# Hybrid decoder step on one core: in the second mixer, both background queues step together at every second tick up to the last head's products

## The chip, the cores and the metric

The kernel runs on one core of one Trainium2 chip. The metric is the device time of one execution in microseconds, the median of three runs. The engines are TensorE (PE in the profile; PEld is its weight load), VectorE (DVE), ScalarE (ACT), GpSimd (POOL) and SyncE (SP, which issues DMAs).

## The reference, cut to what matters

The program computes one inference step of a two-layer trunk of width 1024: layer 0 has a Mamba-2 mixer, layer 1 an HGRN2 mixer, each followed by a squared-ReLU MLP. 512 prompt tokens and 8 sequences of 4 new tokens pass through together, 544 columns in all. The change touches the second mixer, HGRN2, with 8 heads of 128 x 128:

```python
def hgrn_mixer(u, state, lb, w_in, norm_w, w_out):
    proj = (u @ w_in).astype(jnp.float32)
    q = jax.nn.silu(proj[..., :HGRN_F])
    fz = proj[..., HGRN_F:2 * HGRN_F]
    v = proj[..., 2 * HGRN_F:2 * HGRN_F + D_MODEL]
    g = proj[..., 2 * HGRN_F + D_MODEL:]
    logf = ...                                  # from fz and lb
    k = (1.0 - lb) * jax.nn.sigmoid(-fz)
    o, s = hgrn_chunk_scan(q, k, v, logf, state)   # S_t = diag(f_t) S_{t-1} + k_t v_t^T, o_t = S_t^T q_t
    o = group_rmsnorm(o, norm_w, HGRN_N_HEADS) * jax.nn.silu(g)
    return o @ w_out, s
```

## The kernel before, in words

Activations lie transposed, features on the 128 partitions and the 544 tokens along the free dimension. A big product is made in three fp32r passes (high and low halves of weight and activation), each as two matmuls of 272 columns; the weights come in units of 128 x 1024, are split into `whi` and `wlo` by `split` (L198: a cast on ScalarE, a subtraction on VectorE), and `products` (L319) writes them into one of two PSUM tiles `acc`. After every six steps (12 matmuls) `products` calls `tick` (L295).

In the second mixer (`hgrn`, L1175) the foreground is `head` (L1415) for h = 0 to 7: four products (q, f, v, g; four ticks each, so 16 ticks a head) and their evacuations. All the rest of a head is done in two background queues of Python generators, which `tick` advances:

- Queue 0, `levels` (L1231): seven levels s = 1, 2, 4, ... 64. Each issues small score products (`pa`, L1249, L1256, L1268), masks them into `ac` and `att` on VectorE, and multiplies q and K by decays on VectorE (L1279, L1280), which the next level's products read. Between two levels one step is `values` (L1305): transposes of v (`pv`, `pvs`). Each step yields `PACE_LEVELS`, so 8 steps a head.
- Queue 1, `states` (L1330), which `levels` starts when it ends: transposes of K (`pk`), the chunk states (`pS`, then S on VectorE, L1356), the old states' part (`pz`), the outputs (`po`, `pzs`; L1375 to L1380), their norm (squares on ScalarE, L1383; a sum, a Newton iteration of small steps and a scaling to `o2` on VectorE, L1386 to L1392), the two halves of the state update (`pn`, L1396, and four VectorE steps each on `hst`, L1399), the store of `hst`, and at the end transposes of `o2` (`pt`, `pts`; L1406, L1407), the gate `g` (L1410, L1411) and its split into `oh` and `ol`.

The numbers that a step yields are ticks until the next one: `tick` takes 1 from the first entry of each queue, and steps that queue while the entry is not above 0. The two queues keep their own time. Behind the last head come the products of the output projection, `pho` (L1456): half 0 of them reads the gated outputs of heads 0 to 3, half 1 those of heads 4 to 7, and `drain("hs7")` makes what is left of the last head's steps before half 1. They tick too, every 12 matmuls.

All small products share four PSUM tiles (`mx`). The framework below orders each engine's instructions by its own planning of the recorded program, so a matmul may stand a few places from where it was recorded; each engine then runs its list in order.

Of the kernel before, what the change touches and what calls it, by code (L numbers as in the profile page):

```python
# [41 lines left out]


PACE = (1.1, 0.9, 1.4, 0.8)
PACE_LEVELS, PACE_STATES = 1.8, 1.6

U_SSD_IN = 0
U_SSD_OUT = U_SSD_IN + 40
# [53 lines left out]
def trunk(ctx: ExitStack, tc: tile.TileContext, io):  # L102
# [37 lines left out]

    ready = {}
    loaded = {("u", i): t for i, t in enumerate(first)}
    state = {"load": 2, "conv": 0}
    loads = [("u", u) for u in range(U_MLP)]
    jobs = [(("u", u), u) for u in range(U_MLP)]

# [141 lines left out]
    def unit(u):  # L288
        return take(("u", u))
# [3 lines left out]
    queues = [[], []]  # L293

    def tick():  # L295
        for q in queues:
            if q:
                q[0][1] -= 1
                while q and q[0][1] <= 0:
                    step(q)  # L300

    def step(q):
        try:
            q[0][1] += next(q[0][0])
        except StopIteration:
            left = q.pop(0)[1]
            if q:
                q[0][1] += left
# [7 lines left out]
    def drain(name):  # L316
        for q in queues:
            while any(e[2] == name for e in q):
                step(q)  # L319
# [5 lines left out]
    def products(ps, w, ops, first, last, c0=0, step=P, run=0):  # L325

        n = len(ops)
        order = [(k, j) for k in range(n) for j in range(3)]
        run = run or (4 if "w" in sp else 0)
        if run:  # L330

            order = [(k, j) for k0 in range(0, n, run) for js in ((0, 1), (2,)) for k in range(k0, min(k0 + run, n)) for j in js]
        for i, (k, j) in enumerate(order):
            oh, ol = ops[k]
            a, o = ((w[0], oh), (w[0], ol), (w[1], oh))[j]
            for h in range(2):
                nc.tensor.matmul(  # L337
                    ps[:, h, :HF], block(a, c0 + k * step), o[:, h * HF : (h + 1) * HF],
                    start=(first and i == 0), stop=(last and i == len(order) - 1),
                )  # L340
            if i % 6 == 5:
                tick()

    def acc_tile(name):
        return psb.tile([P, 2, 512], F32, tag="acc", name=name)
# [79 lines left out]
    def add_to_x(m, ps, then):  # L425
        with tc.high_priority():
            nc.vector.tensor_tensor(v3(x[m]), ps[:, :, :HF], v3(x[m]), ADD)
        if then is not None:
            then(m)


    def ssd(then):
# [393 lines left out]
        def dt_product():  # L826

            wd = pool.tile([P, KT, NS], F32, tag="E", bufs=2, name="wd")
            nc.vector.tensor_tensor(
                wd, wdt, vec[:, V_NMIX0 : V_NMIX0 + KT].unsqueeze(2).to_broadcast([P, KT, NS]), MUL  # L830
            )
            pd = acc_tile("pd")
            for i in range(2):
                for h in range(2):
                    for c in range(4):
                        k = 4 * i + c
                        nc.tensor.matmul(
                            pd[c * NS : (c + 1) * NS, h, :HF], wd[:, k, :], x[k][:, h * HF : (h + 1) * HF],
                            start=(i == 0), stop=(i == 1), tile_position=(0, c * NS),
                        )  # L840
                tick()
            pdx = pool.tile([P, 640], F32, tag="xs", bufs=5, name="pdx")
            nc.vector.tensor_tensor(v3(pdx[:, :T]), pd[:, :, :HF], v3(rb), MUL)
            nc.gpsimd.tensor_copy(
                pdx[:, T:640].rearrange("p (a b) -> p a b", b=NS), pdx[:, NP_:T].unsqueeze(1).to_broadcast([P, 3, NS])
            )
            return pdx
# [122 lines left out]
    def mlp(name, plan, v0, then, last=False):  # L970
# [105 lines left out]
        def seventh(name_, u):  # L1076
# [11 lines left out]
            for k in range(4):  # L1088
                oh, ol = ops_[name_, k]
                for j, (w, o) in enumerate(((hi, oh), (hi, ol), (lo, oh))):  # L1090
                    nc.tensor.matmul(  # L1091
                        ps, block(w, k * P), o, start=(name_ in ("p1", "p2", "q7") and k == 0 and j == 0),
                        stop=(k == 3 and j == 2), skip_group_check=name_ in ("n6", "n5", "p3", "q4"),
                    )
            tick()
            release(1)
            keep = {"p1": "s1", "n6": "sv", "n5": "sw"}.get(name_)
# [81 lines left out]
    def hgrn(then):  # L1179
# [235 lines left out]
        def head(u, h):  # L1415
            hc = slice(h, h + 1)
            pq, pf = None, None
            if h == 0:
                pq, pf = product(u), product(u + 1)
                drain("hn")  # L1420
            qz = project(u, "qz", pq)
            QQ = pool.tile([P, 2, T], F32, tag="q", name=f"q{h}")
            q, Q = QQ[:, 0], QQ[:, 1]
            nc.scalar.activation(q, qz, AF.Sigmoid)
            nc.vector.tensor_tensor(q, qz, q, MUL)
            fz = project(u + 1, "fz", pf)
            f = pool.tile([P, T], F32, tag="f", name=f"f{h}")
            K = pool.tile([P, 640], F32, tag="K", name=f"K{h}")
            nf = pool.tile([P, T], F32, tag="nf", name=f"nf{h}")
            nc.scalar.activation(f, fz, AF.Sigmoid)  # L1430
            nc.scalar.activation(nf, fz, AF.Sigmoid, scale=-1.0)
            nc.vector.scalar_tensor_tensor(f, nf, lbf[:, hc], f, MUL, ADD)
            nc.vector.tensor_scalar(K[:, :T], nf, olb[:, hc], None, MUL)
            nc.vector.tensor_tensor(Q, q, f, MUL)
            d = {}
            background(levels(h, QQ, K, f, d), f"hl{h}", wait=2.5)
            d["vz"] = project(u + 2, "vz")
            gz = project(u + 3, "gz")
            g = pool.tile([P, T], F32, tag="g", name=f"g{h}")
            nc.scalar.activation(g, gz, AF.Sigmoid)  # L1440
            nc.vector.tensor_tensor(g, gz, g, MUL)
            d["g"] = g

        sc = slice(NP_, T)
        u = U_HGRN_IN
        ops = [[pool.tile([P, T], F32R, tag=f"o{c}{h}", bufs=1, name=f"o{c}{h}") for c in "hl"] for h in range(8)]
        for h in range(8):
            head(u, h)
            u += 4
        for half in range(2):  # L1450
            if half:
                drain("hs7")
            for mp in range(4):
                w = unit(u)
                u += 1
                for i in range(2):  # L1456
                    ps = acc_tile(f"pho{half}_{mp}_{i}")
                    products(ps, w, ops[4 * half : 4 * half + 4], True, True, i * P, 2 * P)
                    add_to_x(2 * mp + i, ps, then if half == 1 else None)
# [50 lines left out]
    ssd(pre_norm(V_NMLP0))  # L1510
    mlp("m0", plans[0], V_NMLP0, pre_norm(V_NMIX1))
    hgrn(pre_norm(V_NMLP1))
    mlp("m1", plans[1], V_NMLP1, last_norm, True)

# [111 lines left out]
def _build(arrays):  # L1626
    import concourse.bacc as bacc

    nc = bacc.Bacc("TRN2", target_bir_lowering=False, num_devices=1)
    io = {n: nc.dram_tensor(f"in_{n}", v.shape, mybir.dt.from_np(v.dtype), kind="ExternalInput").ap() for n, v in arrays.items()}  # L1630
    for n, s in _OUT.items():
        io[n] = nc.dram_tensor(f"out_{n}", s, F32, kind="ExternalOutput").ap()
    with tile.TileContext(nc) as tc:
        trunk(tc, io)
    return nc
# [22 lines left out]
```

## Time and profile before

| | |
|---|---|
| Median of 3 runs | 1518.32 us (1518.02 to 1518.69) |
| The profiled execution | 1517.97 us, its span 1516.2 us |
| TensorE busy over the span | 99% |
| VectorE busy over the span | 83% |
| Second mixer, first small product to last `pt` | 835 to 1123 us of the span |

The profiled execution is 0.35 us below the median. In the rows further down a time is the start in us from the beginning of the span; a row of the timeline merges instructions of the same kind that follow each other (x2 is a pair of 272-column matmuls). Ends of matmuls are modelled, so the starts are what is read.

### The profile page before, as it was taken

How to read it: one execution, taken by the hardware profiler on the slowest of the kernel's cores; microseconds unless marked ns; L12 is line 12 of the kernel's file. 1: busy time of each engine (PE TensorE's matmuls, PEld its weight loads, DVE VectorE, ACT ScalarE, POOL GpSimd, SP SyncE). 2: the span in 40 equal slices, each digit the busy share in tenths (PEclk: the TensorE clock that was granted, in tenths of full speed). 3: DMA queues.
4: the chain of work that ended last, by engine and by line, in shares of the span. 5: the costliest groups of instructions: out<-in, count | busy, mean ns of one | idle time of the engine just before them, and what ended most of it. 6: DMA issues, size and time to landing. Idle time of an engine off the chain costs nothing. (4 is left out here: it accounts for less than half of the span.)

```text
span 1516.2 us, 33224 instructions
## 1 busy us (share of the span) xinstructions
PE 1495.4 (99%) x13144; PEld 1440.3 (95%) x13144; DVE 1261.5 (83%) x2532; ACT 882.3 (58%) x1740; POOL 188.0 (12%) x273
## 2 busy tenths in 40 slices
PE   9999999999999999999999999999999999999997
PEld 7998989898999999999999999999999999999996
DVE  7879798978777989888898788888877989888895
ACT  5685766757346658575676333333336758576673
POOL 3211011110012111111110000000002111111101
PEclk9999999999999999999999999999999999999998
DMA  6366557574466667564754232233228666575741
GB/s 199 106 192 169 148 140 203 130 223 115 114 178 135 141 161 183 145 183 131 191 131 130 74 99 87 87 98 105 86 86 202 133 168 180 140 181 140 184 123 66
DMA packets 105789, 215.46 MB, mean 142 GB/s; under 512 B 16481, under 2 KB 36865, under 8 KB 105633
## 3 DMA queue, kind: packets, MB, share of 16 engines
q1 hardware_dynamic: 81328, 170.24, 34.7%
q0 software_dynamic: 23040, 41.95, 17.3%
q8 instruction: 103, 1.69, 0.5%
q10 hardware_dynamic: 1264, 1.14, 0.2%
q14 instruction: 54, 0.43, 0.1%
HBM read 196.12 MB, written 17.18 MB: 141 GB/s over the span
## 5 line engine op out<-in xcount | busy, mean ns | idle before, releaser
L199 ACT CAST whi<-raw 128x512 fp32r<-128x512 f32 x194 | 119.4, 617 | 212.0 <-PE ps L337 154.6
L200 DVE TENSOR_TENSOR wlo<-raw,whi 128x512 fp32r<-128x512 f32 x194 | 133.8, 691 | 30.8 <-ACT whi L199 28.0
L188 POOL DMA_DIRECT2D v<-in_W x94 | 83.0, 1038 | 463.6 <-DVE fl_p L200 134.0
L337 PE MATMUL ps<-uh_s,whi 128*128 128x272 f32 x576 | 124.3, 297 | 2.5 <-DVE BC L518 2.4
L337 PE MATMUL ps<-ul_s,whi 128*128 128x272 f32 x576 | 120.2, 290 | 0.0
L337 PE MATMUL ps<-uh,whi 128*128 128x272 f32 x512 | 112.6, 300 | 0.0
L337 PE MATMUL ps<-ul,whi 128*128 128x272 f32 x512 | 106.5, 289 | 0.0
L337 PE MATMUL ps<-uh,wlo 128*128 128x272 f32 x512 | 106.3, 289 | 0.0
L337 PEld LDWEIGHTS ps<-uh_s,whi 128*128 128x128 f32 x576 | 90.5, 189 | 8.5 <-issue 6.9
L337 PEld LDWEIGHTS ps<-ul_s,whi 128*128 128x128 f32 x576 | 90.9, 189 | 0.2
L200 DVE TENSOR_TENSOR fl_p<-raw,fh_p 128x512 fp32r<-128x512 f32 x94 | 64.1, 689 | 28.9 <-ACT fh_p L199 25.3
L337 PE MATMUL ps<-uh_s,wlo 128*128 128x272 f32 x576 | 86.4, 290 | 0.0
L337 PEld LDWEIGHTS ps<-uh,whi 128*128 128x128 f32 x512 | 80.8, 189 | 3.7 <-issue 1.4
L337 PEld LDWEIGHTS ps<-ul,whi 128*128 128x128 f32 x512 | 80.4, 189 | 0.0
L337 PEld LDWEIGHTS ps<-uh,wlo 128*128 128x128 f32 x512 | 80.0, 188 | 0.0
L199 ACT CAST fh_p<-raw 128x512 fp32r<-128x512 f32 x94 | 57.6, 620 | 37.9 <-PE pp L1091 19.9
L337 PEld LDWEIGHTS ps<-uh_s,wlo 128*128 128x128 f32 x576 | 78.1, 190 | 1.1 <-issue 0.8
L223 ACT CAST whi<-raw 128x512 fp32r<-128x512 f32 x66 | 40.6, 618 | 49.4 <-PE ps L337 19.6
L511 DVE SCALAR_TENSOR_TENSOR cacc<-pre,vh,cacc 128x568 f32<-128x568 f32 x72 | 57.8, 803 | 7.6 <-ACT cacc L509 7.1
L337 PE MATMUL po<-yh,whi 128*128 128x272 f32 x256 | 55.5, 297 | 1.2 <-ACT yh L199 1.2
L1091 PE MATMUL pp<-m_tl,fh_n 128*128 128x272 f32 x192 | 55.3, 288 | 0.0
L1091 PE MATMUL pc_q<-m_th,fh_q 128*128 128x272 f32 x192 | 55.3, 288 | 0.0
(480 smaller groups left out, 5156.0 us busy)
## 6 DMA issues: line engine op xcount, KB each, us to landing
raw<-in_W SPq DMA_DIRECT2D x175, 512.0 KB, 4.0
v<-in_W SPq DMA_DIRECT2D x94, 256.0 KB, 4.1
v<-in_W POOLq DMA_DIRECT2D x94, 256.0 KB, 5.6
wlo<-in_W POOLq DMA_DIRECT2D x66, 256.0 KB, 6.2
a<-in_W SPq DMA_DIRECT2D x47, 256.0 KB, 4.3
w<-cum_d SPq DMA_DIRECT2D x16, 512.0 KB, 6.9
st<-in_ssm_in SPq DMA_DIRECT2D x16, 512.0 KB, 4.6
out_ssm_s<-st SPq DMA_DIRECT2D x16, 512.0 KB, 6.6
```

Source lines behind the costliest of these rows:

```text
L188: nc.gpsimd.dma_start(raw[:, c : c + 512], io["W"][u + 1][:, :512], accum_op=ADD)
L199: nc.scalar.copy(hi, raw)
L200: (eng or nc.vector).tensor_tensor(lo, raw, hi.bitcast(F32), SUB)
L223: nc.scalar.copy(hi[a], c)
L337: nc.tensor.matmul(ps[:, h, :HF], block(a, c0 + k * step), o[:, h * HF : (h + 1) * HF], start=(first and i == 0), stop=(last and i == len( ...
L511: nc.vector.scalar_tensor_tensor(acc, pre[:, i : i + 568], vh[:, wc + 24 * i : wc + 24 * i + 1], acc, MUL, ADD)
L1091: nc.tensor.matmul(ps, block(w, k * P), o, start=(name_ in ("p1", "p2", "q7") and k == 0 and j == 0), stop=(k == 3 and j == 2), skip_group ...
```

## The change

`tick` counts its calls. A queue still loses 1 per tick, but is stepped only at ticks whose number is a multiple of `beat`. `beat` is 2 from the first head to the last head's own products, and 1 before and behind them. A step of `levels` now yields 2 instead of 1.8.

```diff
-PACE_LEVELS, PACE_STATES = 1.8, 1.6
+PACE_LEVELS, PACE_STATES = 2, 1.6
...
-    state = {"load": 2, "conv": 0}
+    state = {"load": 2, "conv": 0, "ticks": 0, "beat": 1}
...
     def tick():
+
+        state["ticks"] += 1
         for q in queues:
             if q:
                 q[0][1] -= 1
-                while q and q[0][1] <= 0:
+                while q and q[0][1] <= 0 and state["ticks"] % state["beat"] == 0:
                     step(q)
...
         u = U_HGRN_IN
+        state["beat"] = 2
         ops = [[pool.tile([P, T], F32R, tag=f"o{c}{h}", bufs=1, name=f"o{c}{h}") for c in "hl"] for h in range(8)]
         for h in range(8):
             head(u, h)
             u += 4
+        state["beat"] = 1
         for half in range(2):
```

The two programs hold the same instructions on every engine; their order differs from the mixer's first norm (`hn_pc`) on. Lines of the changed kernel are 2 higher than before for L296 to L1445 and 4 higher for what follows `head` in `hgrn`. A run of small products between two big matmuls is called a visit here. From the norm's `hn_pr` to the last `pt` PE's list has 97 visits before and 72 now.

**A head in the middle.** PE's list around the state steps of head 2 and the level steps of head 3 (the first digit in a name is the head's, the last number only counts tiles); first before:

```order
L1249 MATMUL pa3_2_12379<-q3_12194,K3_12284 32x32 x16
L1256 MATMUL pa3_2_12379<-q3_12194,K3_12284 32x32
L1352 MATMUL pS2_12406<-vt2_12120,kt2_12349 128x128 x4
...
L337 MATMUL ps134_12301<-uh7_16_10603,wlo134_1_12202 128x272 x2
L1362 MATMUL pz2_12429<-hst2_12342,qm2_12351 32x128 x8
L1365 MATMUL pz2_12429<-ident_77,K2_11776 128x128
L337 MATMUL ps135_12456<-uh0_16_10131,whi135_0_12293 128x272 x2
...
L1249 MATMUL pa3_4_12469<-q3_12194,K3_12284 32x32 x16
L1375 MATMUL po2_12491<-vt2_12120,att2_11842 128x128 x2
...
L1377 MATMUL po2_12491<-S2_12411,q2_11688 128x128
L1379 MATMUL pzs2_12499<-zi2_12439,h_sel_10632 32x128
L1380 MATMUL pzs2_12499<-vs2_12126,sats2_11843 32x128
L337 MATMUL ps135_12456<-uh2_16_10324,whi135_0_12293 128x272 x2
```

and in the changed kernel:

```order
L1251 MATMUL pa3_2_12428<-q3_12159,K3_12274 32x32 x16
L1258 MATMUL pa3_2_12428<-q3_12159,K3_12274 32x32
L1354 MATMUL pS2_12455<-vt2_12137,kt2_12385 128x128 x4
L339 MATMUL ps135_12403<-uh4_16_10475,whi135_1_12284 128x272 x2
...
L339 MATMUL ps135_12403<-uh7_16_10603,wlo135_1_12286 128x272 x2
L1251 MATMUL pa3_4_12490<-q3_12159,K3_12274 32x32 x16
L1364 MATMUL pz2_12512<-hst2_12378,qm2_12387 32x128 x8
L1367 MATMUL pz2_12512<-ident_77,K2_11753 128x128
L1377 MATMUL po2_12527<-vt2_12137,att2_11830 128x128 x2
...
L1379 MATMUL po2_12527<-S2_12460,q2_11638 128x128
L1381 MATMUL pzs2_12535<-zi2_12522,h_sel_10632 32x128
L1382 MATMUL pzs2_12535<-vs2_12143,sats2_11831 32x128
```

Before, `pz` is a visit of its own, 10 matmuls behind `pS`, and `po` follows 12 matmuls later together with the level's `pa`. Now `pa`, `pz`, `po` and `pzs` are one visit, 24 matmuls behind `pS`, and nothing but `po` stands between `pz` and `pzs`, which reads `zi`, ScalarE's copy of `pz`. All visits of the heads in the middle now have 24 matmuls between them.

**Behind the last head.** PE's list from the last state product of head 7 to the first use of its gated output `oh7`; first before:

```order
L1396 MATMUL pn7_1_15077<-vm7_14897,kq7_14972 128x512
L337 MATMUL pho0_3_1_15064<-oh2_10652,whi155_1_14903 128x272 x2
...
L1406 MATMUL pt7_15097<-ident_77,o27_14998 128x128 x4
L1407 MATMUL pts7_15098<-ident_77,o27_14998 128x32
L337 MATMUL pho1_0_0_15118<-oh4_10656,whi156_0_15024 128x272 x2
...
L337 MATMUL pho1_0_1_15149<-ol5_10659,whi156_0_15024 128x272 x2
L337 MATMUL pho1_0_0_15118<-oh7_10662,whi156_1_15025 128x272 x2
L337 MATMUL pho1_0_1_15149<-oh5_10658,wlo156_0_15026 128x272 x2
...
L337 MATMUL pho1_0_0_15118<-ol7_10663,whi156_1_15025 128x272 x2
L337 MATMUL pho1_0_0_15118<-oh7_10662,wlo156_1_15027 128x272 x2
```

and in the changed kernel:

```order
L339 MATMUL pho0_3_1_15024<-oh3_10654,wlo155_1_14882 128x272 x2
L1398 MATMUL pn7_0_15083<-vm7_14947,kq7_15020 128x512
L1398 MATMUL pn7_1_15090<-vm7_14947,kq7_15020 128x512
L339 MATMUL pho1_0_0_15118<-oh4_10656,whi156_0_14964 128x272 x2
...
L339 MATMUL pho1_0_1_15149<-oh6_10660,wlo156_1_14967 128x272 x2
L1408 MATMUL pt7_15097<-ident_77,o27_15048 128x128 x4
L1409 MATMUL pts7_15098<-ident_77,o27_15048 128x32
L339 MATMUL pho1_0_0_15118<-oh7_10662,whi156_1_14965 128x272 x2
L339 MATMUL pho1_0_1_15149<-oh7_10662,whi156_1_14965 128x272 x2
L339 MATMUL pho1_0_0_15118<-ol7_10663,whi156_1_14965 128x272 x2
...
L339 MATMUL pho1_1_0_15192<-oh4_10656,whi157_0_15110 128x272 x2
```

Before, 12 matmuls stand between `pn7_1` and `pt7`, and 28 between `pts7` and the first matmul that reads `oh7`. Now both `pn7` stand together at the end of half 0, the 36 matmuls of half 1 that need only heads 4 to 6 all stand ahead of `pt7`, and `oh7` is read right behind `pts7`. The third row after that reads `ol7`, and four matmuls later `pho1_1_0` needs the PSUM tile of `pho1_0_0`.

**VectorE at the same place**, from the norm's sum for head 7 to `ol7`; first before:

```order
L1386 TENSOR_REDUCE oms7_15002<-o27_14998 128x5
L1387 TENSOR_SCALAR oms7_15002<-oms7_15002 128x5
...
L1389 TENSOR_TENSOR o27_14998<-po7_14987,nwr_15005 128x512
L200 TENSOR_TENSOR wlo157_0_15112<-raw157_15022,whi157_0_15110 128x512
L1392 TENSOR_SCALAR o27_14998<-pzs7_14995,nwr_15005 32x128
L1399 SCALAR_TENSOR_TENSOR hst7_14886<-hst7_14886,T7_2_14485,pn7_1_15077 128x128 x2
L427 TENSOR_TENSOR x_75<-pho0_3_1_15064,x_75 128x544
L200 TENSOR_TENSOR wlo157_1_15113<-raw157_15022,whi157_1_15111 128x512
L1399 SCALAR_TENSOR_TENSOR hst7_14886<-hst7_14886,T7_2_14485,pn7_1_15077 128x128 x2
L1410 SCALAR_TENSOR_TENSOR g7_14678<-pt7_15097,vec_76,g7_14678 128x512
L1411 SCALAR_TENSOR_TENSOR g7_14678<-pts7_15098,vec_76,g7_14678 128x32
L200 TENSOR_TENSOR ol7_10663<-g7_14678,oh7_10662 128x544
```

and in the changed kernel:

```order
L1388 TENSOR_REDUCE oms7_15052<-o27_15048 128x5
...
L429 TENSOR_TENSOR x_75<-pho0_3_1_15024,x_75 128x544
L200 TENSOR_TENSOR wlo157_1_15113<-raw157_14962,whi157_1_15111 128x512
L366 TENSOR_TENSOR nwt_15056<-nwt_15056,nwm_15057 128x5
L1401 SCALAR_TENSOR_TENSOR hst7_14936<-hst7_14936,T7_2_14534,pn7_0_15083 128x128
...
L1401 SCALAR_TENSOR_TENSOR hst7_14936<-hst7_14936,T7_2_14534,pn7_1_15090 128x128
L1391 TENSOR_TENSOR o27_15048<-po7_15037,nwr_15055 128x512
L200 TENSOR_TENSOR wlo158_0_15186<-raw158_15108,whi158_0_15184 128x512
L1394 TENSOR_SCALAR o27_15048<-pzs7_15045,nwr_15055 32x128
L1412 SCALAR_TENSOR_TENSOR g7_14647<-pt7_15097,vec_76,g7_14647 128x512
L1413 SCALAR_TENSOR_TENSOR g7_14647<-pts7_15098,vec_76,g7_14647 128x32
L200 TENSOR_TENSOR ol7_10663<-g7_14647,oh7_10662 128x544
```

Before, four updates of `hst7` and a weight split stand between `o2`'s scaling and the gate `g7`. Now all eight updates of `hst7` stand within the Newton iteration, alternating with its steps, ahead of the scaling; a weight split (`wlo158_0`) stands between the scaling's two parts, and the gate follows at once.

## Rows read from the trace of the kernel before

**Rows 1.** The page, section 1: busy time of each engine, its share of the span, instructions.

```profile
PE 1495.4 (99%) x13144; PEld 1440.3 (95%) x13144; DVE 1261.5 (83%) x2532; ACT 882.3 (58%) x1740; POOL 188.0 (12%) x273
```

**Rows 2.** First the busy times in one stretch (start:end, length, then each engine's busy time with its instructions, the granted clock of PE, DMA share, GB/s); then, behind the dots, the whole list of PE's waits from 816 us to the end (who waited for whom, us in total, times, longest).

```profile
828.00:1113.00 285.00, 284.91 (x3557) 265.74 (x3556) 232.05 (x645) 98.50 (x210) 8.78 (x22) 1.00 0.28 90
...
PE fn_pr L1496 <- DVE nwr L365: 2.2, 1, 2.2
PE fn_pc L1490 <- ACT sq L1480: 0.9, 1, 0.9
```

**Rows 3.** Timeline of PE, two visits that stand alone: `pa` of one level, and behind the dots `pS`, each with the pair before it and the two pairs behind it. Columns: start, length, what, count.

```profile
946.98 0.41 PE L337 MATMUL ps<-uh,wlo 128*128 128x272 f32 x2
947.33 0.46 PE L1249 MATMUL pa<-q,K 128*32 128x32 f32 x32
947.72 0.52 PE L337 MATMUL ps<-uh,whi 128*128 128x272 f32 x2
948.07 0.42 PE L337 MATMUL ps<-ul,whi 128*128 128x272 f32 x2
...
968.14 0.42 PE L337 MATMUL ps<-uh,wlo 128*128 128x272 f32 x2
968.39 1.05 PE L1352 MATMUL pS<-vt,kt 128*128 128x128 f32 x8
969.20 0.50 PE L337 MATMUL ps<-uh,whi 128*128 128x272 f32 x2
969.54 0.41 PE L337 MATMUL ps<-ul,whi 128*128 128x272 f32 x2
```

**Rows 4.** Timeline of PE, a `pa` (with its two matmuls for the new tokens, L1256) and `pS` in one visit, again from the pair before to the second pair behind.

```profile
935.60 0.42 PE L337 MATMUL ps<-uh,whi 128*128 128x272 f32 x2
935.95 0.46 PE L1249 MATMUL pa<-q,K 128*32 128x32 f32 x32
936.22 0.23 PE L1256 MATMUL pa<-q,K 128*32 128x32 f32 x2
936.38 1.16 PE L1352 MATMUL pS<-vt,kt 128*128 128x128 f32 x8
937.30 0.50 PE L337 MATMUL ps<-ul,whi 128*128 128x272 f32 x2
937.63 0.41 PE L337 MATMUL ps<-uh,wlo 128*128 128x272 f32 x2
```

**Rows 5.** Timeline of PE behind the last head: the first `po` of head 7, the first pair behind `pzs`, `pt`, the first pair that reads `oh7`, and the last pair of `pho1_0_1`.

```profile
1113.12 0.61 PE L1375 MATMUL po<-vt,att 128*128 128x128 f32 x4
...
1115.44 0.52 PE L337 MATMUL pho<-oh,whi 128*128 128x272 f32 x2
...
1122.04 0.60 PE L1406 MATMUL pt<-ident,o 128*128 128x128 f32 x4
...
1126.36 0.41 PE L337 MATMUL pho<-oh,whi 128*128 128x272 f32 x2
...
1128.62 0.41 PE L337 MATMUL pho<-oh,wlo 128*128 128x272 f32 x2
```

**Rows 6.** Timeline of DVE in the same stretch: the norm's sum, two updates of `hst` with a Newton step between them, the scaling's two parts with a weight split between them, the gate's two parts, `ol`, and the evacuation of `pho1_0_1` into x.

```profile
1115.91 0.82 DVE L1386 TENSOR_REDUCE oms<-o 128x5 f32<-128x640 f32 x1 [1.26 <-ACT o L1384]
...
1117.49 0.35 DVE L1399 SCALAR_TENSOR_TENSOR hst<-hst,T,pn 128x128 f32<-128x128 f32 x1
...
1117.83 0.34 DVE L1399 SCALAR_TENSOR_TENSOR hst<-hst,T,pn 128x128 f32<-128x128 f32 x1
...
1120.23 0.69 DVE L1389 TENSOR_TENSOR o<-po,nwr 128x512 f32<-128x512 f32 x1
1120.90 0.69 DVE L200 TENSOR_TENSOR wlo<-raw,whi 128x512 fp32r<-128x512 f32 x1
1121.51 0.33 DVE L1392 TENSOR_SCALAR o<-pzs,nwr 32x128 f32<-32x128 f32 x1
...
1124.04 0.73 DVE L1410 SCALAR_TENSOR_TENSOR g<-pt,vec,g 128x512 f32<-128x512 f32 x1
1124.70 0.23 DVE L1411 SCALAR_TENSOR_TENSOR g<-pts,vec,g 128x32 f32<-128x32 f32 x1
1125.64 0.73 DVE L200 TENSOR_TENSOR ol<-g,oh 128x544 fp32r<-128x544 f32 x1 [0.71 <-ACT oh L199]
...
1129.06 0.72 DVE L427 TENSOR_TENSOR x<-pho,x 128x544 f32<-128x544 f32 x1 [0.48 <-PE pho L337]
```

**Rows 7.** Timeline of ACT in the same stretch: the squares of `po`, and the cast to `oh`.

```profile
1114.88 0.60 ACT L1383 ACTIVATE o<-po 128x512 f32<-128x512 f32 x1 [1.14 <-PE po L1377]
...
1124.96 0.65 ACT L199 CAST oh<-g 128x544 fp32r<-128x544 f32 x1 [2.36 <-DVE g L1411]
```

**Rows 8.** Three stretches behind the first mixer (columns as in the first row of Rows 2), and behind the dots two lines of PE's list of waits over the whole span; their three waits lie between 434 and 439 us.

```profile
434.00:439.00 5.00, 3.12 (x17) 2.04 (x16) 5.00 (x9) 3.63 (x6) 1.75 (x2) 1.00 0.54 175
439.10:442.40 3.30, 3.30 (x16) 3.30 (x16) 0.99 (x2) 0.62 (x1) 0.86 (x1) 0.50 1.05 246
442.50:446.00 3.50, 3.50 (x30) 3.50 (x29) 1.85 (x3) 1.82 (x3) 1.71 (x2) 1.00 1.11 255
...
PE po L337 <- ACT yh L199: 1.2, 2, 0.6
PE po L337 <- DVE yl L200: 0.6, 1, 0.6
```

## The prediction

> **What bounds the kernel.** I read the page's busy times first: TensorE is busy 1495.4 us, 99% of the span [rows 1]. Then the stretch that the change reorders: from 828 to 1113 us PE is busy 284.91 of 285.00 us at a granted clock of 1.00, VectorE 232.05 (81%), ScalarE 98.50 (35%) [rows 2]. Then the list of PE's waits: from 816 us to the end it holds two, of 2.2 and 0.9 us, both in the last layer's norm and none in the mixer [rows 2]. The reader is to see that there is no stall here to remove. PE's matmuls stay the same in number and shape, so the time can change in three ways only: PE spends less or more on going in and out of visits, a wait appears, or the clock falls. Last I read the timelines of the visits [rows 3, 4] and of the end of the last head [rows 5 to 7], where the order changes most.
>
> **Term 1: 25 visits fewer.** The last pair before `pS` starts 0.25 us before it [rows 3], so a 272-column matmul takes 0.126. I price a visit as the time from the last pair before it to the second pair behind it, less the two pairs that fill 0.505 of it. `pa` alone: 948.07 - 946.98 - 0.505 = 0.585. `pS` alone: 969.54 - 968.14 - 0.505 = 0.895 [rows 3]. Together they are 1.48. In one visit they cost 937.63 - 935.60 - 0.505 = 1.525 [rows 4], where `pa` has two small matmuls more. The bounds of what a removed visit is worth: below, nothing, because the row of the merged visit is not under the sum of the two. Above, the change-over at both edges. The pair ahead of `pa` lasts 0.35 instead of 0.25, and so does the first pair behind a visit [rows 3], which makes 0.20 for a visit, 5.0 us for 25. I take 0, since rows 4 show just such a merge at no gain, and keep 5.0 for the range.
>
> What the rows show at an edge is that the entry into `pa` (tiles of 128*32) costs 0.10 more than the entry into `pS` (128*128 like the big matmuls) [rows 3]. The Trainium skill, page "TensorEngine Tiling (Array Packing)", section "Key Properties" under "Tiling Modes", says that a change of the tiling mode, and not merely of the tile, drains the TensorE; the trace agrees at that one edge. By this rule merging `pS` with anything saves nothing, and only a merge of `pz` with `pa` saves one entry, 0.10 in each of some four more heads than before, so that the sum would be 0.4 us lower.
>
> **Term 2: waits in the heads.** All visits there now stand 24 matmuls, 3.0 us, apart. `pzs` reads `zi`, which ScalarE copies from `pz`, and only `po` is left between them. The 8 matmuls of `po` take about 1.7 us (first at 1113.12, ScalarE reads the result at 1114.88 [rows 5, 7]). The copy is smaller than the squares, which take 0.60 [rows 7], and even with a cast of 0.65 [rows 7] ahead of it, it fits into 1.7 us; ScalarE is 65% idle here. So I cost this at 0; without that cover it would be some 0.3 per head. The level steps: VectorE must multiply q and K by the decays between two level visits. Its work is the same, 81% of the time, so 3.0 us leave 0.57 free on average. An instruction of the size of a weight split or of `ol` (0.61 to 0.73 [rows 6]) that lands ahead of the update at the wrong place uses this up. Walking through the new order, I find the update ahead of level 64 the tightest, behind an evacuation, a weight split and `ol`, with about 0.6 us left by the durations of rows like these. I take 0 and keep 0 to 0.73 a head as bounds. No bigger wait in the heads is removed either, since there was none.
>
> **Term 3: behind the last head.** Let 0 be the first `po` of head 7 (1113.12 before). Between `pzs` and `pt` PE has 48 matmuls and the two `pn` in both orders, so it would again reach `pt` at 1122.04 - 1113.12 = 8.92 [rows 5]. From `pt` to the first use of `oh7` it took 4.32 with 28 matmuls (3.53) between [rows 5], so `pt`, `pts` and the change-over are 0.79. Now `oh7` follows at once. Without a wait PE would read it at 9.7 and, two pairs later, `ol7` at 10.2.
>
> VectorE's chain to `ol7`, each duration as the distance to what follows:
> - The sum starts at 2.79 as before (1115.91). Four small steps and one more follow, and at about 4.2 the evacuation of `pho0_3_1` (its last pair starts at 2.32 + 0.35 + 4 x 0.25 = 3.7; an evacuation that waits for PE starts 0.44 behind the pair: 1129.06 - 1128.62 [rows 5, 6]), 0.7; then the split `wlo157_1`, 0.61. That makes 5.5.
> - Eight updates of `hst7`, each with a Newton step, at 0.34 (1117.83 - 1117.49): 2.7, to 8.2. These had stood in part behind the scaling; now PE's `pt` waits behind all eight.
> - The scaling's first part, 0.67, to 8.9, just in time for `pt`. Then `wlo158_0`, 0.61, to 9.5, if ScalarE's cast for it is done in time, and the second part, 0.26, to 9.75 [rows 6]. Only then can `pts` go, and the gate start.
> - The gate's two parts start 0.66 apart, the cast to `oh` 0.26 behind the second, `ol` 0.68 behind the cast, and it takes 0.73 [rows 6, 7]: 9.75 + 0.66 + 0.26 + 0.68 + 0.73 = 12.1.
>
> So PE reads `ol7` at 12.1 instead of 10.2: a wait of **1.9 us** in all, first at `oh`, then at `ol`. Before, 28 matmuls hid this. What is late next: four matmuls after `ol7` comes `pho1_1_0`, which needs the PSUM tile of `pho1_0_0`. Its last pair starts at 12.35, its evacuation at 12.8 and ends at 13.5, where PE would be ready at 13.1: another **0.4 us**. Before, the ten matmuls of `pho1_0_1` and more stood between. Bounds of this term: 1.0 if the chain runs half a us earlier at two of its links, 3.2 if ScalarE's cast is late and the DVE chain slips by one more split. I take 2.3.
>
> The time from there on is PE's own, so the delay stays to the end; the two later waits on the last norm [rows 2] move with PE.
>
> The Python count itself and the move of `PACE_LEVELS` add no instruction, no DMA and no queue entry on SP or POOL; loads of weights stand in the same sequence by units, and the stretch moves 90 GB/s at a DMA share of 0.28 [rows 2], which is cover enough.
>
> **Sum.** 0 + 0 + 1.9 + 0.4 = +2.3 us. The profiled execution takes 1517.97, so 1520.27; it lies 0.35 below the median of 1518.32, so the predicted median is **1520.6 us**. A measurement of this kernel tells about 0.2%, 3.0 us, from no change, so 1515.3 to 1521.4 count as the same.
>
> **Rivals.**
> - *The clock falls behind the new wait.* After three waits of 0.6 us each within 434 to 439 us the granted clock was 0.50 (1.2 of 2.4 GHz) from 439.1 to 442.4, where PE did 16 matmuls in 3.3 us instead of 30 in 3.5 [rows 8]: 3.3 - 16 x 0.117 = 1.4, about 1.5 us. The new wait is of the same total but in two pieces with matmuls around, and PE was nowhere else idle. It gives 1522.1.
> - *VectorE is late once a head* (the slower side). Both queues now issue their steps at one tick, so level masks, decays and the state's work bunch. The place is level 64's `pa`, the point from which it decides is VectorE's work between two visits passing 3.0 us. Price: between 0 and 0.73 a head, I take 0.5 in 7 heads, 3.5 us: 1524.1. For it: only 0.57 us are free on average. Against: the walk found 0.6 left at the tightest place, and PE had no wait at all before.
> - *Visits pay after all.* If each of the 25 saves both change-overs, -5.0 + 2.3 gives 1515.6; without the tail's wait 1513.3, faster. Against it stand rows 4.
> - *The change does nothing that shows.* If the framework's other waits or a faster chain hide the tail (the bound of 1.0 or less, and a few tenths saved at visits), the time stays at 1518.3.
>
> **Chances.** Forecast 0.58, clock 0.13, VectorE late 0.08, visits pay 0.10, nothing shows 0.11. The range 1517.5 to 1523.0 holds the forecast with its bounds, the fallen clock and the case without effect; it leaves out VectorE late and visits that pay, 0.18. Faster by over 0.2%: rather more than half of the visits' case, 0.06. Slower by over 0.2%: the clock and VectorE's case, and 0.06 of the forecast's upper end, 0.27. The same: 0.67.
>
> **What would show it.** In the changed kernel's profile the list of PE's waits should hold one or two entries at the end of the mixer, on `oh`, `ol`, the scaling of `o` or the evacuation into x, about 2.3 us together, and none in the heads. `pt` should start near 8.9 behind the first `po` of head 7, the pair that reads `oh7` near 11.4 and `ol7`'s near 12.1. Visits should cost what the sums of their parts cost, so that PE's busy time in the mixer stays within 0.5 us. A granted clock under 1.00 behind the tail would be the first rival; waits at `pa` in every head the second. I am wrong if the mixer gets shorter by more than 2 us, or if no wait shows at its end.

## The result

| | before | changed |
|---|---|---|
| Median of 10 runs | 1518.37 us (1517.30 to 1520.04) | 1520.80 us (1519.04 to 1523.20) |
| Ratio of the runs | | 1.0017 (95%: 1.0009 to 1.0025) |
| The profiled execution's span | 1516.2 us | 1521.4 us |

The change costs about 2.4 us (1.4 to 3.8 by the interval): a small loss, but clear of the scatter of the runs. The profiled execution of the change is the slowest of its ten. The forecast was 1520.6. The total was hit; the experiments below show that one of its parts, the price of the visits, was not, and that a fall of the clock and, it seems, a later weight behind the mixer took back most of that error.

### The profile page after: what moved, and what is told of

It reads as the page before. It is cut to its first block, busy times and chain, and to the rows that moved or that the text cites. A ratio compares the mean times of both kernels' runs of the same rounds, so it can differ in the third digit from the quotient of the medians.

```text
span 1521.4 us, 33204 instructions
## 1 busy us (share of the span) xinstructions
PE 1496.4 (98%) x13144; PEld 1440.1 (95%) x13144; DVE 1268.3 (83%) x2532; ACT 881.7 (58%) x1740; POOL 191.1 (13%) x273
```

## The profile after

PE is still the busy engine (the page, section 1), but its list of waits from the mixer's end on, which held two entries before [rows 2], now holds six. The page first, then that list (who waited for whom, us in total, times, longest):

```profile
PE 1496.4 (98%) x13144; PEld 1440.1 (95%) x13144; DVE 1268.3 (83%) x2532; ACT 881.7 (58%) x1740; POOL 191.1 (13%) x273
```

```profile
PE fn_pr L1500 <- DVE nwr L367: 2.2, 1, 2.2
PE pho L339 <- ACT oh L199: 1.2, 1, 1.2
PE fn_pc L1494 <- ACT sq L1484: 0.9, 1, 0.9
PE pm L339 <- DMA wlo<-in_W: 0.7, 1, 0.7
PE pho L339 <- DVE x L429: 0.3, 1, 0.3
PE pts L1409 <- DVE o L1394: 0.2, 1, 0.2
```

The `oh`, `x` and `pts` entries are the forecast wait behind the last head, 1.8 us in three pieces (1.22, 0.32 and 0.25 in the timeline below). None lies in the heads. The one on `wlo`'s DMA was not forecast. The timeline of PE at the mixer's end answers to [rows 5] (first `po` of head 7, first pair behind `pzs`, `pt`, `pts`, the pairs that read `oh7`, then `ol7`, and the first pair of `pho1_1_0`):

```profile
1118.74 0.61 PE L1377 MATMUL po<-vt,att 128*128 128x128 f32 x4
...
1121.06 0.52 PE L339 MATMUL pho<-oh,whi 128*128 128x272 f32 x2
...
1127.72 0.63 PE L1408 MATMUL pt<-ident,o 128*128 128x128 f32 x4
1128.60 0.21 PE L1409 MATMUL pts<-ident,o 32*128 32x32 f32 x1 [0.25 <-DVE o L1394]
1130.03 0.77 PE L339 MATMUL pho<-oh,whi 128*128 128x272 f32 x4 [1.22 <-ACT oh L199]
1130.79 0.52 PE L339 MATMUL pho<-ol,whi 128*128 128x272 f32 x2
...
1132.37 0.52 PE L339 MATMUL pho<-oh,whi 128*128 128x272 f32 x2 [0.32 <-DVE x L429]
```

And VectorE's chain, as in [rows 6]: first and last update of `hst`, the scaling with a weight split inside, the gate, `ol`.

```profile
1121.53 0.82 DVE L1388 TENSOR_REDUCE oms<-o 128x5 f32<-128x640 f32 x1 [1.49 <-ACT o L1386]
...
1124.31 0.34 DVE L1401 SCALAR_TENSOR_TENSOR hst<-hst,T,pn 128x128 f32<-128x128 f32 x1
...
1126.63 0.34 DVE L1401 SCALAR_TENSOR_TENSOR hst<-hst,T,pn 128x128 f32<-128x128 f32 x1
1126.89 0.69 DVE L1391 TENSOR_TENSOR o<-po,nwr 128x512 f32<-128x512 f32 x1
1127.51 0.69 DVE L200 TENSOR_TENSOR wlo<-raw,whi 128x512 fp32r<-128x512 f32 x1
1128.12 0.33 DVE L1394 TENSOR_SCALAR o<-pzs,nwr 32x128 f32<-32x128 f32 x1
1128.39 0.75 DVE L1412 SCALAR_TENSOR_TENSOR g<-pt,vec,g 128x512 f32<-128x512 f32 x1
1129.06 0.24 DVE L1413 SCALAR_TENSOR_TENSOR g<-pts,vec,g 128x32 f32<-128x32 f32 x1
1130.01 0.72 DVE L200 TENSOR_TENSOR ol<-g,oh 128x544 fp32r<-128x544 f32 x1 [0.71 <-ACT oh L199]
```

Counted from the first `po`, with the forecast behind it: `pt` 8.98 (8.9), `pts` 9.86 (9.75), `oh7` 11.29 (11.4), `ol7` 12.05 (12.1), `pho1_1_0` 13.63 (13.5). The listed waits, 1.8 us, are fewer than the 2.3 forecast; PE loses the rest around them, mostly because the first pair behind a wait takes 0.35 us or more instead of 0.25 (1130.79 to 1131.14, 1132.37 to 1132.73). The reader is to see that VectorE does not pause between `hst` and `g`: the wait is a full chain of small work that lost its 28 covering matmuls.

**Where the 5.2 us between the two profiled spans lie.** I cut the span at two events that both programs have: the first pair of the second layer's first product (`ps`) and the first `m_pc`, the norm ahead of the last MLP. Rows of the timeline of PE, before and then changed:

```profile
816.08 0.41 PE L337 MATMUL ps<-uh,whi 128*128 128x272 f32 x2
...
1151.47 1.17 PE L373 MATMUL m_pc<-ones,ssq 128*128 128x1 f32 x10
```

```profile
818.90 0.41 PE L339 MATMUL ps<-uh,whi 128*128 128x272 f32 x2
...
1155.08 1.17 PE L375 MATMUL m_pc<-ones,ssq 128*128 128x1 f32 x10
```

Ahead: 816.08 and 818.90, 2.82 us, in a part where PE's orders do not differ; in the change's five profiles this event lies between 815.90 and 818.90, so it is scatter. The mixer's stretch: 335.39 and 336.18, only **0.8 us**. Behind: to the ends of the spans 364.70 and 366.35 (end at 1516.17 and 1521.43), 1.65 us. So in this profile the stretch that the change reorders explains a third of the 2.4 us, though its wait is there in full. I cut it once more at the first `po` of head 7 and take 0.12535 us for each 272-column matmul from both parts, since the changed order has 36 of them more ahead of that `po` (1716 instead of 1680; 1728 in e6). Unbroken runs of such matmuls in the mixer start 0.1255 to 0.1259 us apart, which would move the differences in the table by some 0.02. "Heads" is all from the first `ps` to that `po`, the mixer's norm included:

| kernel | stretch | heads, less big matmuls | behind the last head, less big matmuls | behind `m_pc` |
|---|---|---|---|---|
| before; again (e9) | 335.39; 335.38 | 86.45; 86.45 | 3.75; 3.75 | 364.70; 365.10 |
| changed; e4; e10 | 336.18; 336.15; 336.19 | 84.74; 84.71; 84.74 | 6.25; 6.25; 6.26 | 366.35; 365.04; 365.39 |
| changed, e8; e11 | 337.25; 337.25 | 84.70; 84.71 | 7.36; 7.35 | 366.37; 365.52 |
| e1 pace 2 alone | 340.04 | 87.51 | 7.35 | 365.26 |
| e2 beat alone | 334.47 | 85.54 | 3.75 | 365.34 |
| e3; e7 last head faster | 333.62; 333.65 | 84.71; 84.74 | 3.73; 3.73 | 365.33; 364.71 |
| e5 queues apart | 338.82 | 87.37 | 6.26 | 365.37 |
| e6 beat through half 0 | 338.58 | 85.07 | 8.32 | 365.67 |

The heads became 1.7 us cheaper (forecast 0), the end of the last head 2.5 us dearer (forecast 2.3). The stretch repeats to 0.05 us from profile to profile, so one profile decides on it, while the total scatters by some us. The two rows of the change differ only by a fall of the clock behind the last head, which comes further down.

## The experiments

Theory A: the change saves 1.7 us by merged visits in the heads and loses 2.5 us behind the last head, and the loss comes with the pace of 2, not with the beat. Rivals: the wait comes from stepping the queues together (B); merged visits are worth nothing, as I had forecast (C).

**The pace alone (e1)**: the kernel before with

```diff
-PACE_LEVELS, PACE_STATES = 1.8, 1.6
+PACE_LEVELS, PACE_STATES = 2, 1.6
```

> The kernel before with PACE_LEVELS 2 and no beat. Its list has 98 visits (before 94, the change 72, counted from hn_pr to the last pts), and behind the last head it is that of the change: 36 matmuls of half 1 ahead of pt, oh7 read right behind pts. The mixer's stretch (first pair of the second layer's first product to the first m_pc) is 335.4 us before and 336.2 in the change. Theory A (the wait behind the last head costs 2.5 and comes with the pace alone; merged visits save 1.7): waits at pts, oh7 and the evacuation into x together 1.8 or so, stretch 337.9 to 338.2, total 1520.5 to 1521.3, slower than the change's own mixer. Theory B (the wait comes from stepping both queues together): no wait, stretch 335.4, total 1518.4. Theory C (visits are worth nothing, as forecast, and the wait costs only 0.8 net): stretch 336.2.

Measured: 1523.61 us, ratio 1.0030 (1.0020 to 1.0040); stretch 340.04. The waits at `pts` (0.3) and `oh7` (1.2) are there without any beat, so theory B is out. The size is 2 us over theory A, in two parts. The heads cost 1.06 more than before: `pvs`, `pz` and `pv` stand alone more often among its 98 visits (97 before, by the count used for the two kernels). And behind the wait the granted clock fell, which answers to [rows 8]; one stretch of this kernel (columns as there):

```profile
1132.00:1134.00 2.00, 2.00 (x10) 1.77 (x9) 1.82 (x4) 1.83 (x4) 0.00 (x0) 0.50 0.00 0
```

Its part behind the last head is 7.35 instead of 6.25.

**The beat alone (e2)**: the change with

```diff
-PACE_LEVELS, PACE_STATES = 2, 1.6
+PACE_LEVELS, PACE_STATES = 1.8, 1.6
```

> The change with PACE_LEVELS 1.8: 75 visits, and behind the last head the order of before (28 matmuls between pts7 and oh7). Theory A (merged visits save 1.7, the wait comes with the pace): no wait in the mixer, stretch 333.7 to 334.0 against 335.4 before, total 1516.5 to 1517.2. Theory B (the wait comes from stepping the queues together): stretch 336 or more with a wait at oh7. Theory C (visits are worth nothing): 335.4, total 1518.4.

Measured: 1517.93 us, ratio 0.9996 (0.9988 to 1.0005), stretch 334.47. Behind the last head it costs what before costs, 3.75, with no wait: the wait is the pace's. The heads save 0.9, between A and C. They have the seven merges that pay (below), but give back two things: one `pn` waits 0.4 for ScalarE's `vt` and costs 0.84 instead of 0.23 by the count used below, and in three heads `pts` stands apart from `pt`, one matmul behind it, at some 0.07 each. In total the kernel can't be told from before.

**Head 7 faster (e3, e7)**: the change with head 7's level steps at 1.8 and state steps at 1.2:

```diff
-                yield PACE_LEVELS
+                yield 1.8 if h == 7 else PACE_LEVELS
...
         def states(h, d):
-
+            pace = 1.2 if h == 7 else PACE_STATES
...
-            yield PACE_STATES
+            yield pace
```

and so at every yield of the two generators.

> The change with head 7's level steps at 1.8 and its state steps at 1.2: 72 visits, heads 0 to 6 as in the change, and 27 matmuls between pts7 and oh7. Theory A: no wait behind the last head, stretch 333.7, total 1516.3 to 1517.0, below both kernels. Theory C (visits are worth nothing): 335.4, total 1518.4. If the state steps at 1.2 crowd VectorE behind the last head, a wait at pt of up to 1 us.

> The change with head 7's levels at 1.8 and states at 1.2 once more, for more runs. Stretch 333.6 again (before 335.39). If the total follows the stretch: median 1516.5 to 1517.5. If the change's program loses elsewhere what it gains here: 1518.5 as the first time.

Measured: stretch 333.62 and 333.65, 1.75 under before. The whole list of PE's waits from 816 us on is that of before again, with line numbers moved (e3):

```profile
PE fn_pr L1500 <- DVE nwr L367: 2.2, 1, 2.2
PE fn_pc L1494 <- ACT sq L1484: 0.9, 1, 0.9
```

Heads of the change, end of before: the two parts come apart as theory A says. In total 1518.68 us the first time (ratio 0.9996, 0.9987 to 1.0005) and 1516.66 the second (0.9990, 0.9982 to 0.9999). The stretch is shorter for sure; that the whole program is faster, only the second set of runs shows.

**Queues apart (e5)**: the change with each queue on its own half of the beat:

```diff
-                while q and q[0][1] <= 0 and state["ticks"] % state["beat"] == 0:
+                while q and q[0][1] <= 0 and (state["ticks"] + (q is queues[1])) % state["beat"] == 0:
```

> The change with queue 0 stepped at even and queue 1 at odd ticks: each queue keeps its beat of 2 and its 24 matmuls, but their visits stand apart, 109 instead of 72. The order behind the last head is that of the change. Theory A (merged visits save): pz alone again at 0.833 instead of 0.546 within a visit of pa and po, pvs and pk alone, so the mixer's stretch is 338.4 to 339.4 against 336.15 in the change, with the same waits at pts, oh7 and x of 1.8. Rival (what the change saved in the heads comes from the spacing of the steps, and merging is worth nothing, as forecast): 336.2.

Measured: 1522.13 us, ratio 1.0026 (1.0015 to 1.0037), stretch 338.82, the end unchanged at 6.26 and the heads 2.7 dearer. The spacing of each queue's steps is kept here, so the heads' saving comes from merging, not from spacing. Rival C falls.

Which merge pays is seen in rows. `pz` alone in the kernel before, and behind the dots its visit of `pa`, `po` and `pzs`, each from the last pair ahead to the second behind:

```profile
938.39 0.41 PE L337 MATMUL ps<-uh,wlo 128*128 128x272 f32 x2
938.73 0.64 PE L1362 MATMUL pz<-hst,qm 128*32 128x128 f32 x16
...
939.72 0.41 PE L337 MATMUL ps<-ul,whi 128*128 128x272 f32 x2
...
940.73 0.41 PE L337 MATMUL ps<-uh,wlo 128*128 128x272 f32 x2
941.07 0.46 PE L1249 MATMUL pa<-q,K 128*32 128x32 f32 x32
...
944.24 0.41 PE L337 MATMUL ps<-ul,whi 128*128 128x272 f32 x2
```

The changed kernel, the visit of all four:

```profile
946.58 0.41 PE L339 MATMUL ps<-uh,wlo 128*128 128x272 f32 x2
946.92 0.46 PE L1251 MATMUL pa<-q,K 128*32 128x32 f32 x32
947.20 0.66 PE L1364 MATMUL pz<-hst,qm 128*32 128x128 f32 x16
...
950.64 0.41 PE L339 MATMUL ps<-ul,whi 128*128 128x272 f32 x2
```

Less the 0.505 of two pairs: `pz` 0.825, `pa po pzs` 3.005, all four 3.555. So `pz` adds 0.55 where it follows `pa`, and 0.28 is saved, in 7 heads. With `pS` instead, in the kernel with the queues apart, nothing is:

```profile
942.42 0.41 PE L339 MATMUL ps<-uh,wlo 128*128 128x272 f32 x2
942.67 1.05 PE L1354 MATMUL pS<-vt,kt 128*128 128x128 f32 x8
943.66 0.64 PE L1364 MATMUL pz<-hst,qm 128*32 128x128 f32 x16
...
944.65 0.41 PE L339 MATMUL ps<-ul,whi 128*128 128x272 f32 x2
```

944.65 - 942.42 - 0.505 = 1.725, the sum of 0.895 [rows 3] and 0.825. `pa` and `pz` share the tiles of 128*32 and `pS` does not. I read this as the change into such tiles and back being paid once instead of twice; the rows show the sum saved, not its two halves. Before, three heads already had `pa` and `pz` in one visit (0.33 saved in each by the same count), so this merge gives 7 x 0.28 - 3 x 0.33 = 1.0 of the 1.7. The rest is 0.04 to 0.07 a time at `pk`, `pn` and `pt`, and 0.17 once at `hn_pc` of the mixer's norm, ahead of the heads: its visit costs 1.29 in both profiles of the kernel before and 1.12 in the change, where it follows another pair of the same product. That 0.17 is no merge, and the kernel with the queues apart has it too.

**The beat through half 0 (e6)**: the return to 1 moved behind half 0 of the output projection:

```diff
-        state["beat"] = 1
         for half in range(2):
             if half:
+                state["beat"] = 1
                 drain("hs7")
```

> The change with the beat of 2 kept through half 0 of the output projection: 69 visits; pz, po, pzs and both pn of head 7 in one visit, then 36 matmuls to pt, so PE reaches pt 12 matmuls (1.5 us) earlier against the same chain on VectorE. If the wait is that chain less PE's work ahead of it: waits at the mixer's end of 1.8 + 1.5 = 3.3, stretch 337.3 to 337.8. If the wait has a fixed price whatever stands ahead: 336.0. If the granted clock falls to 0.50 behind the longer wait, 1.1 to 1.5 more.

Measured: 1524.51 us, ratio 1.0042 (1.0029 to 1.0055), stretch 338.58. PE's waits in the mixer:

```profile
PE pho L339 <- ACT oh L199: 1.5, 1, 1.5
PE pt L1408 <- DVE o L1391: 1.3, 1, 1.3
...
PE pn L1398 <- ACT vt L1315: 0.4, 1, 0.4
```

The first two are at the mixer's end, 2.8 us against 3.3 forecast; the third lies in the heads, at a `pn`, as in e2. The clock fell here too (a mean of 0.85 from 1130 to 1140), and then the wait on the evacuation into x is missing. So the fair comparison is with a profile of the change in which the clock fell (e8 below), whose waits at `pts` and `oh7` are 0.3 and 1.2: 12 matmuls less ahead of `pt`, 1.5 us of work, make the wait 1.3 longer. The wait is VectorE's chain less the matmuls that stand ahead, not a fixed price, which would have given 336.0. The fall of the clock takes about 1.1 of the 338.58 by the price below; without it the stretch is the 337.5 of the forecast.

**The same kernels again (e4, e8, e10, e11, e9)**: no edit, for more profiles.

> The change once more, for a second profile. In its first profile 2.8 us were lost ahead of the mixer, where nothing differs, and 1.6 behind it, 0.86 of them at one wait for a weight's DMA. If these are scatter of one execution: stretch 336.2 again, and from m_pc to the end about 364.7 as before. If the loss behind the mixer belongs to the change: 366 again. Total 1520 to 1521.

> The change a third time. Stretch 336.15 if the granted clock stays at 1.00 behind the wait on oh7, 337.3 if it falls to 0.50 there as in the profile of the pace alone (1131.5 to 1134.9). Total 1519.5 to 1521.

> The change, for a fourth profile. Stretch 336.15, or 337.3 if the granted clock falls to 0.50 behind the wait on oh7 (in one profile of the change out of three). If the later loads make the loss behind the mixer: SP's load 1.5 us ahead of m_pc, and a wait for a weight's DMA of 0.3 to 1.1 us some 15 us behind m_pc in about two of three executions, 366 from m_pc to the end; if those waits were scatter, none and 365.

> The change, for a fifth profile. Stretch 336.15, or 337.3 if the granted clock falls to 0.50 behind the wait on oh7; SP's load 1.5 us ahead of m_pc. With a wait for a weight's DMA some 15 us behind m_pc the end comes 366 us behind m_pc, without it 365.

> The kernel before, for a second profile. Stretch 335.4 with no wait; from m_pc to the end 364.7 to 365.4 with no wait for a weight's DMA; the first load behind the mixer's end on SP's queue 2.8 us ahead of m_pc as in its first profile (1.5 ahead in all six profiles that have the wait on oh7).

Measured: the change takes 1519.96 us, 1.0013 of before (1.0004 to 1.0022), in e4 and 1521.23, 1.0021 (1.0012 to 1.0029), in e8; the others are single executions. The table above has the stretches. Two things show only over several profiles.

First, behind the same waits at `pts` and `oh7` the clock stays at 1.00 in three profiles of the change and falls to 0.50 in two (e8, e11). Of the three variants with a wait there it falls in e1 and e6 and not in e5. What decides it is not shown. Two stretches of e8, and then one of the first profile:

```profile
1129.00:1131.00 2.00, 2.00 (x9) 1.72 (x9) 1.86 (x4) 1.99 (x4) 0.00 (x0) 0.50 0.00 0
1131.00:1133.00 2.00, 2.00 (x15) 2.00 (x14) 1.85 (x3) 1.01 (x2) 0.00 (x0) 0.79 0.54 152
```

```profile
1133.00:1135.00 2.00, 2.00 (x19) 2.00 (x18) 1.85 (x3) 1.91 (x4) 0.00 (x0) 1.00 0.18 25
```

A fall costs 1.1 us (7.36 - 6.25; under the 1.5 of the forecast, and the list of waits then lacks the 0.3 on the evacuation into x).

Second, behind the mixer. SP's first load there, relative to `m_pc`, comes 2.8 us ahead in all five profiles without the wait on `oh7` and 1.5 ahead in all eight with it. Before, and then changed (SP's queue in the timeline):

```profile
1148.68 13.94 SPq L178 DMA_DIRECT2D raw<-in_W  x3
```

```profile
1153.59 5.58 SPq L178 DMA_DIRECT2D raw<-in_W  x2
```

1151.47 - 1148.68 = 2.79 and 1155.08 - 1153.59 = 1.49. Some 15 us behind `m_pc` PE waits 0.3 to 1.1 for `wlo`'s DMA in four of the eight (two of the change's five) and in none of the five. Neither of the two profiles taken to tell (e10, e11) has it. From `m_pc` to the end the means are 365.73 (the change's five) and 365.04 (the five without).

The traces say more than this count. The weight that PE waits for is issued 4.03 us behind `m_pc` in all thirteen profiles; its issue with the time from there to landing, in the first profile of the change and then before:

```profile
wlo<-in_W POOLq DMA_DIRECT2D x1, 256.0 KB, 11.6
```

```profile
wlo<-in_W POOLq DMA_DIRECT2D x1, 256.0 KB, 10.1
```

It lands 14.4 to 16.1 us behind `m_pc` in the eight profiles and 13.5 to 14.3 in the five, without overlap. PE is ready for it at 15.0 (1170.77, where it starts in the first profile, less the wait of 0.71 and the `m_pc` of 1155.08), and waits in just the four where it lands later. So the later landing belongs to the order with the wait on `oh7`, and the wait is what is left of it where the scatter takes it past 15.0. The transfers issued ahead of it differ in order as well (SP's load comes between GpSimd's in the five and behind them in the eight). No run moved the loads alone, so which of them delays it stays open.

## Why the total was right, and which steps were not

- **What bounds the kernel**: right. PE's own time, a wait and the clock were the ways it could go, and all three went.
- **Term 1, the visits**: wrong in size, 1.7 us saved against 0 forecast, within the 0 to 5.0 kept for the range. The failed step is taking rows 4, the merge of `pa` with `pS`, for all merges. It is right for that one (1.52 by the same count in the change, where `pa` alone with its two matmuls more is 0.63 and `pS` 0.89), but the changed order rests on another merge, `pa` with `pz`, which gives 0.28. The prediction's own sign, that visits cost the sums of their parts, fails there. The Trainium skill, page "TensorEngine Tiling (Array Packing)", section "Key Properties", says that a change of the tiling mode drains the TensorE. The rows agree: `pz` saves beside `pa` and nothing beside `pS`. The prediction named this merge beside its sum, at 0.10, the entry that rows 3 show, without the way back, and kept 0 in the sum; at 0.28 the four heads more would have come to 1.1, two thirds of the 1.7.
- **Term 2, waits in the heads**: right, none in the change's five profiles. VectorE late once a head did not occur. (`po` has 7 matmuls, not 8; the 1.7 us, read from starts, does not depend on it.)
- **Term 3, behind the last head**: right, 2.5 against 2.3 at a clock of 1.00, each event within 0.15 us. Listed waits make 1.8 of it where the forecast had 2.3, and the slow pairs around them the rest. (`pho1_1_0` comes four pairs behind `ol7`, not four matmuls; the forecast's 13.1 counts the pairs.) The runs of e1 and e2 show what the prediction did not say: the wait belongs to the pace of 2, not to the beat.
- **The first rival, the clock**: it is no case apart: it fell in two of the change's five profiles, at 1.1 us. As a mean that is 0.4 us.
- **The loads as "cover enough"**: not upheld behind the mixer, where one weight lands later in every profile with the wait on `oh7` and PE waits for it in two of the change's five. The means behind `m_pc` differ by 0.7 us; that is the cost only if five profiles stand for the runs.
- **The sum**: -1.7 + 2.5 + 0.4 + 0.7 = 1.9 us, where the forecast had 0 + 2.3. The three sets of runs give 2.6, 2.0 and 3.2 (ratios 1.0017, 1.0013, 1.0021, each uncertain by some 1.3 us). So the total was hit in part by luck: the visits were 1.7 too dear, and the clock, the loads and the last head together 1.3 too cheap. The 0.7 us between this sum and the mean of the three sets stays unassigned, within the uncertainty of the runs.

## What to carry to other kernels

Ask of a merge of small products which tile shapes meet in it: here the pair that shares a shape other than its surroundings' saved 0.28 us a time, and the other merges under 0.1. Check the end of a software pipeline by itself when a pace is altered: steady heads gained here, and the last one lost more, because the planner put all covering matmuls ahead of the chain instead of behind it. Where a total scatters, cut the span at events that both programs share; the piece repeated to 0.05 us while the total scattered by several.

## What the runs showed of the hardware that was not expected

The same two waits, 0.25 and 1.2 us with one small product between them, are followed by a fall of the granted clock to 0.50 in some executions and not in others (two of five profiles of one program). The mean clock of an execution goes with its time within one program: of 32 runs of the kernel before, the eleven at a mean clock of 0.995 took 1517.9 us in the mean, the six at 0.993 took 1520.2.
